# Small matmul groups of attention gathered into fewer places between weight chunks

## The chip, the cores and the metric

The kernel runs on one core of a Trainium2 chip. The metric is the device time of one execution in microseconds (us). TensorE (PE) multiplies matrices, ScalarE (ACT) and VectorE (DVE) work on its results and on its operands, SyncE (SP) issues transfers. Each of them runs its own list of instructions in order; an instruction waits where it needs another engine's result or a buffer that is not free yet.

## The reference

One layer of a hybrid decoder trunk on 256 positions of width 2048, in fp32. A convolution branch and differential attention share one input projection and one output projection; then come a 4-head cross attention to 256 memory tokens and a gated feed-forward part. What the change touches is the attention and the preparation of the memory tokens:

```python
logits = einsum("bqnd,bknd->bnqk", q_blk, k) * scale + bias      # 8 heads, two maps each
p = softmax(where(causal, logits, NEG_INF))
w = p[:, :, 0] - lam * p[:, :, 1]                                # one weight matrix per head
d = einsum("bhqk,bkhe->bqhe", w, v)                              # values
d = rms_norm(d, subln_g) * (1.0 - lambda_init)                   # per head, then reshaped
x = x + concatenate([a, d]) @ w_out
m = rms_norm(mem, g_mem); ckv = m @ w_ckv                        # memory tokens
x = x + cross_attention(rms_norm(x, g_cross) @ w_cq, ckv) @ w_co
x = x + (silu(u1) * u2) @ w_down                                 # u: hf @ w_up, then a short convolution
```

## The kernel before

Each fp32 operand of a large product is split into two parts: a rounded one ("hi", a cast on ScalarE, L162) and the rest ("lo", a subtraction on VectorE, L163). Three products of these parts stand for the fp32 product. Weights come in chunks of 512 KB, 128 x 1024; `weight` (from L144 on) issues the transfer and makes hi and lo. Raw, hi and lo have four buffers each, so the cast of a chunk needs the hi buffer of the chunk four before it, that is the end of that chunk's matmuls.

One chunk is twelve wide matmuls (L216, `part_a`), and this is called a step. At the end of each step `stage()` runs what was planned for it with `at(step, ...)`. So the small matmuls of attention stand in groups behind the last wide matmul of a chunk. Steps 32 to 39 are the first half of the values' projection (v0), 40 to 71 q and k of four pairs of heads (qk0 to qk3), 72 to 79 the second half of the values (v1), 80 to 87 and 88 to 95 the memory tokens' keys (ck) and values (cv), and from 96 on the output projection (wo).

The order on TensorE is the order of the code. On the other engines a scheduler places each instruction by its own simulation of the timeline, so a change of the code's order also moves theirs.

Small work of one head, in order: `turn` transposes q and k (L462, L463) and copies them (L465, qkT); `scores` multiplies them (L474, L477, lg), adds the bias on VectorE and takes exponentials on ScalarE (L487, L); `combine` transposes the head's weights (L506, wt) and copies them (L508, wT); `values` multiplies them with v (L519 to L521, o), and ScalarE reads the result four times, twice to scale and twice to square (L524, L526, jk); `sub_turn` scales the normed output (L540), transposes it (L541, oT) and splits it into the mix (L180, L181). The tiles wt, qkT, o, oT, and those of the two norms and of the memory keys' transposes, share two PSUM buffers (tag "sm", L83), so each needs the one two before it to have been read. lg has one buffer.

The table STEPS (L53) gives the step of each planned piece, the table PAIR (L59) the offset from the pair's base 48 + 8b of `turn`, `scores` and `combine` for the pair's two heads. Token rows of the memory for its norm (L573, row00 to row11) and quarters of the memory (L560, mem0 to mem3) are transfers of 512 KB on the same queue as the weights, into four buffers that they share with the attention's outputs (tag "h4"); a row is squared in place on ScalarE (L574), a quarter is split (L180, L181).

Of the kernel before, what the change touches and what calls it, by code (L numbers as in the profile page):

```python
# [27 lines left out]
NH = 8  # L28
# [14 lines left out]
for _name, _w in (("g_mix", KT), ("g_mem", KT), ("g_cross", KT), ("g_ffn", KT), ("caw", CT * TAPS),  # L43
# [8 lines left out]

STEPS = dict(x_square=(2, 4, 7, 8), x_add=(5, 7, 9), stats=9, gated=(12, 22, 24, 36), bias=43, lam=46,  # L53
             mem_load=(56, 59, 65, 70), mem_split=(68, 80), mem_square=(78, 72, 75, 81), mem_stats=85,
             mem_turn=(95, 89), ln_sum=80, ln_mean=85, ln_var=89, ln_norm=91,
             values=(59, 60, 67, 67, 81, 88, 85, 84), sub_scale=(69, 92), sub_turn=(72, 75, 90, 80, 94, 95, 92, 95),
             cross_scale=131, cross_logits=132, cross_turn=134, cross_values=135)

PAIR = ((2, "turn", 0), (3, "scores", 0), (3, "turn", 1), (4, "scores", 1), (10, "combine", 1), (8, "combine", 0))  # L59

RATES = ((0, 3.8), (36, 4.1), (46, 3.4))
AHEAD = (3, 0)
# [5 lines left out]
def trunk_kernel(ctx, tc, xT_d, memT_d, mem_d, par_d, tab_d, hot_d, gf_d, wa_d, wck_d, wv_d, wqk_d,  # L68
# [63 lines left out]
    def at(i, f, *args):  # L132
        assert i >= step[0]
        plan.setdefault(i, []).append(partial(f, *args))
# [409 lines left out]
    def attend(b, qk):  # L544

        for i, f, n in PAIR:
            i, hd = 48 + 8 * b + i, 2 * b + n
            if f == "turn":
                at(i, turn, hd, qk)
            else:  # L550
                at(i, scores if f == "scores" else combine, hd)
# [46 lines left out]
    for b in range(2):  # L598
        attend(b, pair(b))
# [5 lines left out]
    for f in (flush, ln_sum):  # L605
        at(STEPS["ln_sum"], f)
    attend(2, pair(2))
    attend(3, pair(3))
    at(STEPS["ln_mean"], ln_mean)
    at(STEPS["ln_var"], ln_var)  # L610
# [415 lines left out]
```

## Time and profile before

| | us |
|---|---|
| median of three runs (lowest, highest) | 1184.17 (1183.75, 1185.91) |
| the profiled execution | 1182.44 |
| its span, first to last instruction | 1180.7 |
| TensorE busy in the span | 1169.5 (99%) |
| VectorE, ScalarE busy | 927.0 (79%), 711.0 (60%) |
| TensorE's share of the chain that ended last | 98% |

The span is the profiled execution without some 1.7 us around it. In a timeline each row is an instruction, or several alike one after another ("x3"), with its start and duration; the brackets at the end of a row tell how long the engine stood idle before it and whose instruction ended that. Matmuls overlap, so what one costs is read from the start of one row to the start of the next.

### The profile page before, as it was taken

To read this page: it belongs to the slowest core of one execution; us is meant where nothing else is said; L and a number is where in the kernel's file an instruction comes from. 1 tells how busy PE (TensorE), PEld (TensorE's weight loads), DVE (VectorE), ACT (ScalarE), POOL (GpSimd) and SP (SyncE) were. 2 spreads that over 40 slices of the span, in tenths; PEclk is the share of its full clock that TensorE was granted. 3 is DMA by queue.
4 is the path that set the end of the run, shared out by engine and by line. 5 is a ranking of instruction groups with operands and counts; after the bars stand their busy time and mean duration, and the time that the engine had idled before them with its cause. 6 is when DMAs were issued, how large, how long until landed. Compare 5 with 4: busy or idle time off the path is not lost.

```text
span 1180.7 us, 17026 instructions
## 1 busy us (share of the span) xinstructions
PE 1169.5 (99%) x6186; PEld 1000.3 (85%) x6186; DVE 927.0 (79%) x1503; ACT 711.0 (60%) x1144; POOL 6.2 (1%) x16
## 2 busy tenths in 40 slices
PE   9999999999999999999999999999999999999997
PEld 7888888788888898888888888888888888888886
DVE  7899999996766687978778778778778877777773
ACT  8654467978655665755555555555555756555553
POOL 0000000000000000000000000000000000000000
PEclk9999999999999999999999999999999999999999
DMA  8756766664666547666566666666666566666663
GB/s 323 220 188 194 199 179 205 214 203 154 195 189 190 176 129 228 185 192 193 183 192 193 185 193 190 186 195 188 189 194 185 188 191 186 196 185 191 195 192 111
DMA packets 64032, 226.33 MB, mean 192 GB/s; under 512 B 7659, under 2 KB 8460, under 8 KB 63820
## 3 DMA queue, kind: packets, MB, share of 16 engines
q1 hardware_dynamic: 62732, 223.25, 60.8%
q0 software_dynamic: 784, 1.34, 0.5%
q8 instruction: 48, 0.79, 0.3%
q10 hardware_dynamic: 432, 0.66, 0.2%
q14 instruction: 36, 0.29, 0.1%
HBM read 222.83 MB, written 2.38 MB: 191 GB/s over the span
## 4 chain that ended last, share of the span: by engine, by line
PE 98%; DMA 1%; ACT 1%; DVE 0%; issue 0%; SPq 0%
PE up L197 27%; PE up L198 14%; PE qk L216 7%; PE a L216 7%; PE acc L846 7%; PE acc L848 7%; PE acc L847 7%; PE wo L197 5%; PE v L216 4%; PE wo L198 3%; PE cv L216 2%; PE ck L216 2%; PE cq L197 1%; PE wc L754 1%; PE cq L198 1%; PE wc L755 1%
## 5 line engine op out<-in xcount | busy, mean ns | idle before, releaser
L197 PE MATMUL up<-hf,hi_up 128*128 128x512 f32 x1408 | 488.3, 391 | 0.0
L198 PE MATMUL up<-hf,lo_up 128*128 128x256 f32 x1408 | 393.9, 280 | 0.0
L197 PEld LDWEIGHTS up<-hf,hi_up 128*128 128x128 f32 x1408 | 263.2, 187 | 57.7
L162 ACT CAST hi_up<-raw_up 128x1024 fp32r<-128x1024 f32 x176 | 185.5, 1054 | 149.3 <-PE up L197 107.6
L163 DVE TENSOR_TENSOR lo_up<-raw_up,hi_up 128x1024 fp32r<-128x1024 f32 x176 | 215.6, 1225 | 74.9 <-ACT hi_up L162 66.5
L198 PEld LDWEIGHTS up<-hf,lo_up 128*128 128x128 f32 x1408 | 266.0, 189 | 0.2
L846 PE MATMUL acc<-hi_dn,gq 128*128 128x512 f32 x352 | 137.3, 390 | 0.0
L848 PE MATMUL acc<-hi_dn,gq 128*128 128x512 f32 x352 | 137.0, 389 | 0.0
L847 PE MATMUL acc<-lo_dn,gq 128*128 128x512 f32 x352 | 137.0, 389 | 0.0
L163 DVE TENSOR_TENSOR lo_dn<-raw_dn,hi_dn 128x1024 fp32r<-128x1024 f32 x88 | 107.9, 1226 | 25.2 <-ACT hi_dn L162 24.9
L347 DVE SCALAR_TENSOR_TENSOR y<-ga,par,y 128x249 f32<-128x249 f32 (+17 forms) x240 | 99.4, 467 | 0.0
L162 ACT CAST hi_dn<-raw_dn 128x1024 fp32r<-128x1024 f32 x88 | 92.1, 1047 | 7.9 <-PE acc L848 6.4
L197 PE MATMUL wo<-mix,hi_wo 128*128 128x512 f32 x256 | 89.3, 395 | 0.0
L216 PE MATMUL qk<-hi_qk,h 128*128 128x512 f32 x256 | 82.3, 394 | 0.0
L216 PE MATMUL a<-hi_a,h 128*128 128x512 f32 x256 | 79.6, 392 | 1.1 <-ACT h L180 1.1
L848 PEld LDWEIGHTS acc<-hi_dn,gq 128*128 128x128 f32 x352 | 66.1, 188 | 13.9
L847 PEld LDWEIGHTS acc<-lo_dn,gq 128*128 128x128 f32 x352 | 66.1, 188 | 13.6
L846 PEld LDWEIGHTS acc<-hi_dn,gq 128*128 128x128 f32 x352 | 66.1, 188 | 13.5
L838 ACT CAST gq<-g_a 128x512 fp32r<-128x512 f32 x64 | 39.4, 623 | 58.6 <-PE acc L847 58.6
L198 PE MATMUL wo<-mix,lo_wo 128*128 128x256 f32 x256 | 70.6, 278 | 0.0
L228 ACT COPY corr_up<-up 128x256 f32<-128x256 f32 x88 | 32.7, 372 | 61.6 <-PE up L198 61.6
L839 DVE TENSOR_TENSOR gq<-g_a,gq 128x512 fp32r<-128x512 f32 x64 | 44.0, 691 | 27.4 <-ACT gq L838 27.4
(261 smaller groups left out, 1747.1 us busy)
## 6 DMA issues: line engine op xcount, KB each, us to landing
raw_up<-in_wup SPq DMA_DIRECT2D x176, 512.0 KB, 4.2
raw_dn<-in_wdn SPq DMA_DIRECT2D x88, 512.0 KB, 3.5
raw_qk<-in_wqk SPq DMA_DIRECT2D x32, 512.0 KB, 3.7
raw_wo<-in_wo SPq DMA_DIRECT2D x32, 512.0 KB, 3.6
raw_a<-in_wa SPq DMA_DIRECT2D x30, 512.0 KB, 4.2
raw_v<-in_wv SPq DMA_DIRECT2D x16, 512.0 KB, 3.5
raw_ck<-in_wck SPq DMA_DIRECT2D x8, 512.0 KB, 3.9
raw_cv<-in_wck SPq DMA_DIRECT2D x8, 512.0 KB, 3.6
```

The lines of the kernel that those rows point to most:

```text
L162: rounded = A.copy(out=hi, in_=raw)
L163: fill(rounded, V.tensor_tensor(out=lo, in0=raw, in1=hi.bitcast(F32), op=ALU.subtract))
L197: T.matmul(tiles[n], hi[:, o:o + P], acts(k), start=begin, stop=False)
L198: T.matmul(tiles[n][:, 0:S] if narrow else tiles[n][:, S:], lo[:, o:o + P], acts(k)[:, 0:S], start=False, stop=end)
L216: T.matmul(tiles[t], a, b[:, w], start=k + j == 0, stop=k == KT - 1 and j == 2)
L228: A.copy(out=c, in_=pst[:, S:])
L347: V.scalar_tensor_tensor(out=y[:, j, s:], in0=gated[j][:, 0:S - s], scalar=w, in1=y[:, j, s:], op0=ALU.mult, op1=ALU.add)
L838: A.copy(out=g[:, :, 0:S], in_=src)
L839: V.tensor_tensor(out=g[:, :, S:], in0=src, in1=g[:, :, 0:S].bitcast(F32), op=ALU.subtract)
L846: T.matmul(acc[t], ah, hi, start=False, stop=False)
L847: T.matmul(acc[t], ah, lo, start=False, stop=False)
L848: T.matmul(acc[t], al, hi, start=False, stop=c == NC - 1 and kk == 1)
```

## The change

Two tables of steps change. The transposes of the weights of a pair's even head move from offset 8 to 11, that is next to the scores of the following pair, and to 10 for the last pair, where they join those of the odd head. The values of heads come in twos: steps 60, 68, 80 and 84 in place of 59, 60, 67, 67, 81, 88, 85 and 84. The transposes of outputs move to 76, 76, 85, 89, 93, 93, 94 and 94, the scalings to 70 and 88, and one transpose of the memory keys from 89 to 91.

```diff
--- before.py
+++ after.py
@@ -52,11 +52,11 @@
 
 STEPS = dict(x_square=(2, 4, 7, 8), x_add=(5, 7, 9), stats=9, gated=(12, 22, 24, 36), bias=43, lam=46,
              mem_load=(56, 59, 65, 70), mem_split=(68, 80), mem_square=(78, 72, 75, 81), mem_stats=85,
-             mem_turn=(95, 89), ln_sum=80, ln_mean=85, ln_var=89, ln_norm=91,
-             values=(59, 60, 67, 67, 81, 88, 85, 84), sub_scale=(69, 92), sub_turn=(72, 75, 90, 80, 94, 95, 92, 95),
+             mem_turn=(95, 91), ln_sum=80, ln_mean=85, ln_var=89, ln_norm=91,
+             values=(60, 60, 68, 68, 80, 80, 84, 84), sub_scale=(70, 88), sub_turn=(76, 76, 85, 89, 93, 93, 94, 94),
              cross_scale=131, cross_logits=132, cross_turn=134, cross_values=135)
 
-PAIR = ((2, "turn", 0), (3, "scores", 0), (3, "turn", 1), (4, "scores", 1), (10, "combine", 1), (8, "combine", 0))
+PAIR = ((2, "turn", 0), (3, "scores", 0), (3, "turn", 1), (4, "scores", 1), (10, "combine", 1), (11, "combine", 0))
 
 RATES = ((0, 3.8), (36, 4.1), (46, 3.4))
 AHEAD = (3, 0)
@@ -544,7 +544,7 @@
     def attend(b, qk):
 
         for i, f, n in PAIR:
-            i, hd = 48 + 8 * b + i, 2 * b + n
+            i, hd = 48 + 8 * b + min(i, 10 if b == NH // 2 - 1 else 11), 2 * b + n
             if f == "turn":
                 at(i, turn, hd, qk)
             else:
```

In TensorE's list the places with small work of steps 50 to 95 become 21 from 27. The wide matmuls stay as they were. On the other engines the scheduler orders the same instructions anew; the transfer of mem1 and its four splits move from the attention's end to the first phase, behind mem0, and all other pieces stay within a few steps.

On ScalarE from step 74 on, before: `row01` and `row10` are squares of token rows, `qkT6` and `qkT7` the copies of `turn`, `wT5` a copy of `combine`, `mix2` with `oT1` an output's split.

```order
L162 CAST hi_v1_6_2330<-raw_v1_6_2328 128x1024
L508 COPY wT5_2187<-wt5_2183 128x384
L465 COPY qkT6_2194<-qkT6_2189 128x512
L574 ACTIVATE row01_2135,part_888<-row01_2135 128x1024
L162 CAST hi_v1_7_2354<-raw_v1_7_2352 128x1024
L180 ACTIVATE mix2_885<-oT1_2218,par_69 128x256
L574 ACTIVATE row10_2257,part_888<-row10_2257 128x1024
L465 COPY qkT7_2255<-qkT7_2250 128x512
```

The same stretch now.

```order
L162 CAST hi_v1_6_2330<-raw_v1_6_2328 128x1024
L574 ACTIVATE row01_2122,part_888<-row01_2122 128x1024
L508 COPY wT5_2174<-wt5_2170 128x384
L465 COPY qkT6_2181<-qkT6_2176 128x512
L540 ACTIVATE o4_0_1709<-o4_0_1709,ro0_2055 128x128 x8
L162 CAST hi_v1_7_2354<-raw_v1_7_2352 128x1024
L508 COPY wT4_2209<-wt4_2205 128x384
L574 ACTIVATE row10_2243,part_888<-row10_2243 128x1024
L465 COPY qkT7_2241<-qkT7_2236 128x512
```

The eight scalings of outputs (L540) and the copy wT4 came in ahead of qkT7's copy, and the output's split left. The transfer of row10 is now released by the square of row01; before, it was released by the splits of mem2 on VectorE.

On ScalarE up to the scaled values (L400, which the values of heads 4 to 7 read), before.

```order
L574 ACTIVATE row00_2349,part_888<-row00_2349 128x1024
L162 CAST hi_ck_0_2381<-raw_ck_0_2379 128x1024
L487 ACTIVATE L6_0_2232,st6_0_2234<-L6_0_2232,st6_0_2234 128x128 x2
L487 ACTIVATE L6_1_2241,st6_1_2243<-L6_1_2241,st6_1_2243 128x256 x2
L162 CAST hi_ck_1_2445<-raw_ck_1_2443 128x1024
L487 ACTIVATE L7_0_2289,st7_0_2291<-L7_0_2289,st7_0_2291 128x128 x2
L162 CAST hi_ck_2_2478<-raw_ck_2_2476 128x1024
L487 ACTIVATE L7_1_2298,st7_1_2300<-L7_1_2298,st7_1_2300 128x256 x2
L400 ACTIVATE v_882<-v1_0_2097,rx_tok_98 128x512
L643 ACT_TABLE_LOAD
L643 ACTIVATE warm_90<-st7_1_2300 128x1
L400 ACTIVATE v_882<-v1_1_2098,rx_tok_98 128x512
```

And now, from the first output's split (oT0) on; ahead of these rows, behind qkT7's copy, stand the table load, the exponentials of head 6 and the cast hi_ck_0.

```order
L180 ACTIVATE mix2_885<-oT0_2268,par_69 128x256
L180 ACTIVATE m2_2400<-mem2_1846,par_69 128x256 x4
L180 ACTIVATE m3_2417<-mem3_2066,par_69 128x256
L180 ACTIVATE mix2_885<-oT1_2275,par_69 128x256
L180 ACTIVATE m3_2417<-mem3_2066,par_69 128x256 x3
L574 ACTIVATE row00_2349,part_888<-row00_2349 128x1024
L487 ACTIVATE L7_0_2289,st7_0_2291<-L7_0_2289,st7_0_2291 128x128 x2
L162 CAST hi_ck_1_2454<-raw_ck_1_2452 128x1024
L487 ACTIVATE L7_1_2298,st7_1_2300<-L7_1_2298,st7_1_2300 128x256 x2
L162 CAST hi_ck_2_2475<-raw_ck_2_2473 128x1024
L400 ACTIVATE v_882<-v1_0_2097,rx_tok_98 128x512
L400 ACTIVATE v_882<-v1_1_2098,rx_tok_98 128x512
```

The eight splits of mem2 and mem3 (L180) moved in here; before they stood ahead of the cast hi_v1_6.

On ScalarE around the weights' copies of the last pair, before.

```order
L162 CAST hi_ck_4_2520<-raw_ck_4_2518 128x1024
L180 ACTIVATE mix2_885<-oT3_2400,par_69 128x256
L508 COPY wT6_2441<-wt6_2437 128x384
L162 CAST hi_ck_5_2548<-raw_ck_5_2546 128x1024
L162 CAST hi_ck_6_2599<-raw_ck_6_2597 128x1024
L508 COPY wT7_2498<-wt7_2494 128x384
L162 CAST hi_ck_7_2617<-raw_ck_7_2615 128x1024
L524 ACTIVATE o4_4_2461<-o4_2463,st4_0_1939 128x128
L526 ACTIVATE jk4_0_2468,oss4_2462<-o4_2463,st4_0_1939 128x128
L524 ACTIVATE o4_4_2461<-o4_2463,st4_1_1948 128x128
L526 ACTIVATE jk4_1_2471,oss4_2462<-o4_2463,st4_1_1948 128x128
L162 CAST hi_cv_0_2641<-raw_cv_0_2639 128x1024
```

Now.

```order
L162 CAST hi_ck_5_2561<-raw_ck_5_2559 128x1024
L162 CAST hi_ck_6_2609<-raw_ck_6_2607 128x1024
L524 ACTIVATE o4_4_2430<-o4_2432,st4_0_1919 128x128
L526 ACTIVATE jk4_0_2437,oss4_2431<-o4_2432,st4_0_1919 128x128
L524 ACTIVATE o4_4_2430<-o4_2432,st4_1_1928 128x128
L526 ACTIVATE jk4_1_2440,oss4_2431<-o4_2432,st4_1_1928 128x128
L524 ACTIVATE o4_4_2430<-o5_2442,st5_0_1992 128x128
L526 ACTIVATE jk5_0_2447,oss4_2431<-o5_2442,st5_0_1992 128x128
L524 ACTIVATE o4_4_2430<-o5_2442,st5_1_2001 128x128
L526 ACTIVATE jk5_1_2450,oss4_2431<-o5_2442,st5_1_2001 128x128
L508 COPY wT7_2495<-wt7_2491 128x384
L508 COPY wT6_2501<-wt6_2497 128x384
```

The reads of heads 4 and 5 (`o4_4` is the tile of heads 4 to 7's outputs) moved ahead of the copies wT7 and wT6, and stand behind the cast hi_ck_6.

On TensorE at the end of chunk ck_2, step 82, before.

```order
L216 MATMUL ck1_2378<-hi_ck_2_2478,m1_2106 128x512
L506 MATMUL wt7_2494<-ident_75,L7_0_2289 128x128
L506 MATMUL wt7_2494<-ident_75,L7_1_2298 128x128 x2
L216 MATMUL ck0_2377<-hi_ck_3_2502,m1_2106 128x512
L216 MATMUL ck0_2377<-lo_ck_3_2503,m1_2106 128x512
```

Now.

```order
L216 MATMUL ck1_2378<-hi_ck_2_2475,m1_2106 128x512
L506 MATMUL wt7_2491<-ident_75,L7_0_2289 128x128
L506 MATMUL wt7_2491<-ident_75,L7_1_2298 128x128 x2
L506 MATMUL wt6_2497<-ident_75,L6_0_2218 128x128
L506 MATMUL wt6_2497<-ident_75,L6_1_2227 128x128 x2
L216 MATMUL ck0_2377<-hi_ck_3_2505,m1_2106 128x512
```

Behind wt7 there is now wt6, which stood at step 80 before; the values of heads 4 and 5, whose buffers these two take, stand at the end of step 80.

## Rows read from the trace of the kernel before

**Rows 1.** The page: busy times with their share, and the clock in 40 slices.
```profile
PE 1169.5 (99%) x6186; PEld 1000.3 (85%) x6186; DVE 927.0 (79%) x1503; ACT 711.0 (60%) x1144; POOL 6.2 (1%) x16
...
PEclk9999999999999999999999999999999999999999
```

**Rows 2.** All waits of TensorE: us in total, times, longest.
```profile
PE a L216 <- ACT h L180: 1.1, 1, 1.1
...
PE qkT L462 <- ACT jk L526: 0.2, 1, 0.2
```

**Rows 3.** ScalarE's timeline, steps 82 to 84: start, us, instruction, [idle before, releaser].
```profile
255.24 1.05 ACT L162 CAST hi_ck<-raw_ck 128x1024 fp32r<-128x1024 f32 x1 [2.38 <-PE ck L216]
...
258.32 1.05 ACT L162 CAST hi_ck<-raw_ck 128x1024 fp32r<-128x1024 f32 x1 [1.66 <-PE ck L216]
259.28 0.36 ACT L524 ACTIVATE o<-o,st 128x128 f32<-128x128 f32 x1
...
260.38 0.21 ACT L526 ACTIVATION_READ_ACCUMULATOR jk<-o,st 128x1 f32 x1
```

**Rows 4.** ScalarE's timeline, steps 71 to 80.
```profile
217.43 2.44 ACT L540 ACTIVATE o<-o,ro 128x128 f32<-128x128 f32 x8
...
224.40 1.71 ACT L180 ACTIVATE m<-mem,par 128x256 fp32r<-128x256 f32 x4
...
229.86 0.48 ACT L508 COPY wT<-wt 128x384 f32<-128x384 f32 x1
...
233.80 1.06 ACT L574 ACTIVATE row<-row 128x1024 f32<-128x1024 f32 x1 [0.20 <-DMA row<-in_mem]
...
234.85 0.57 ACT L465 COPY qkT<-qkT 128x512 f32<-128x512 f32 x1
237.30 1.06 ACT L574 ACTIVATE row<-row 128x1024 f32<-128x1024 f32 x1 [1.87 <-DMA row<-in_mem]
...
238.35 1.04 ACT L162 CAST hi_ck<-raw_ck 128x1024 fp32r<-128x1024 f32 x1
239.30 0.39 ACT L487 ACTIVATE L<-L,st 128x128 f32<-128x128 f32 x1
...
241.06 1.04 ACT L162 CAST hi_ck<-raw_ck 128x1024 fp32r<-128x1024 f32 x1
...
245.11 0.69 ACT L400 ACTIVATE v<-v,rx_tok 128x512 f32<-128x512 f32 x1
245.81 1.28 ACT L643 ACT_TABLE_LOAD   x1
```

**Rows 5.** TensorE's timeline, steps 74 to 83.
```profile
228.40 0.49 PE L506 MATMUL wt<-ident,L 128*128 128x128 f32 x3
...
236.43 0.49 PE L474 MATMUL lg<-qkT 64*128 64x128 f32 x4
...
248.31 0.38 PE L541 MATMUL oT<-ident,o 128*128 128x128 f32 x2
...
252.20 0.47 PE L216 MATMUL ck<-hi_ck,m 128*128 128x512 f32 x1
252.51 0.39 PE L216 MATMUL ck<-lo_ck,m 128*128 128x512 f32 x1
...
255.04 0.49 PE L506 MATMUL wt<-ident,L 128*128 128x128 f32 x3
255.28 0.48 PE L216 MATMUL ck<-hi_ck,m 128*128 128x512 f32 x1
```

**Rows 6.** ScalarE's timeline, first phase.
```profile
32.08 1.05 ACT L162 CAST hi_a<-raw_a 128x1024 fp32r<-128x1024 f32 x1 [0.99 <-DMA raw_a<-in_wa]
34.46 1.05 ACT L162 CAST hi_a<-raw_a 128x1024 fp32r<-128x1024 f32 x1 [1.33 <-PE a L216]
```

**Rows 7.** The DMA queue's timeline, the transfers of token rows.
```profile
229.78 0.33 SPq L573 DMA_DIRECT2D row<-in_mem  x1
...
231.90 0.33 SPq L573 DMA_DIRECT2D row<-in_mem  x1
```

## Prediction

> **What bounds the kernel now.** I read the page first, then the list of TensorE's waits, then the timelines of TensorE, ScalarE and the DMA queue around the steps that the change touches. The page has TensorE busy for 1169.5 of 1180.7 us and its granted clock at full level in every slice [rows 1]. Its longest wait is 1.1 us, at the very start; in the whole attention part it waits once, 0.2 us for a PSUM buffer [rows 2]. So the work in front of TensorE is hidden today, and a change can win only what stands on TensorE itself, and lose whatever it uncovers on ScalarE, VectorE and the queue. The reader is to see in each timeline how near the cover is to its end: on ScalarE the casts of weights wait in brackets for TensorE, which means that ScalarE is ahead there [rows 3], and elsewhere it runs without a gap [rows 4].
>
> **The change part by part.** All small instructions stay; 27 groups of them become 21.
>
> *What is removed.* After a group the first wide matmul takes 0.31 us to the next one (252.20 to 252.51) against 0.23 in the ordinary rhythm (252.51 to 255.04 is eleven of them) [rows 5]. That is at most 0.08 per group, 0.5 for six; a group's own first instruction overlaps the matmul before it, so some of it stays within the larger group, and I take half, 0.25. The one wait of 0.2 [rows 2] goes too, because there values of a pair stood directly ahead of a turn and no longer do. Sum -0.45, carried on as -0.4, between 0 and -0.7.
>
> *Moved early.* The transfer of a quarter of the memory tokens (mem1) now stands before a weight chunk of the first phase, and its four splits before a cast there. Four splits are 1.71 us, as at 224.40 [rows 4]. In that phase ScalarE waits 0.99 us for a weight transfer and, two casts later, 1.33 for TensorE to free a buffer [rows 6]: it is a full round of four buffers ahead, and that cast's chunk is multiplied three chunks of about 2.8 us later. A delay of 1.7 to 3 us is inside that. I take 0, bounds 0 and 0.5.
>
> *Steps 58 to 72.* Values of heads 0 to 3 move back by at most a step and meet no tighter neighbour; the scaling of outputs leaves ScalarE's path at 217.43 (2.44 for the eight) [rows 4] and comes back in step 75. I take 0.
>
> *Step 76.* Here the second output transpose and the scores of head 7 wait for the copy of head 7's transposed q and k (qkT7), since outputs and qkT share two PSUM buffers. Before that copy ScalarE now has, in order: cast hi_v1_6, square of row01, copies wT5 and qkT6, eight scalings, cast hi_v1_7, copy wT4, square of row10. The cast follows the end of step 74's matmuls (228.40 in the trace) [rows 5] by 0.20, as 255.24 does 255.04 [rows 3, 5]. Then 0.95 (238.35 to 239.30) + 1.05 (233.80 to 234.85) + 0.4 + 0.5 (copies of 0.48 and 0.57, each 0.1 into the next) + 2.44 + 0.95 + 0.4 + 1.05 + 0.57 [rows 4] = 8.5 us after that end. Also row10's transfer now waits until row01's square is done, 2.2 after the end, and takes 4.0 (229.78 to 233.80) to 5.4 (231.90 to 237.30) [rows 4, 7]; with its square and the copy behind it, that path ends after 7.8 to 9.2. TensorE reaches the second transpose 8.35 after the same end: 228.40 to 236.43 is 8.03 [rows 5], and wt4 in place of an output transpose and one more transpose ahead add 0.3. Wait 0.15 to 0.9. I take 0.6; bounds 0 (the transfer quick, ScalarE a little ahead) and 2.0 (the transfer another 1 us late, as row00's was against row10's).
>
> *Step 80.* The values of heads 4 and 5 need the scaled v (L400), and now stand at the end of step 80 where head 4's stood one step later and head 5's eight. ScalarE reaches those two instructions, counted from the end of the qkT7 copy, after: table load 1.28, exponentials of head 6 1.76 (239.30 to 241.06), cast 0.95, eight splits of mem2 and mem3 3.3, two of the mix 0.75, square of row00 1.05, exponentials of head 7 1.76, two casts 1.9, v 0.69 = 13.4, and the second v 0.6 later, 14.0 [rows 4]. The splits are what is new: they ran at 224.40 to 229 in before [rows 4], in time that nobody waited for. TensorE gets there 0.3 (the second output transpose, a row of 0.38 that overlaps the next) + (248.31 - 236.43 = 11.88) = 12.2 after the same copy [rows 5]. The first matmuls wait 1.2, the ones on the second v a little more. I take 1.3; bounds 0 (the copy done earlier than TensorE wants it) and 2.5 (each of the 20 instructions 0.05 slower).
>
> *Step 82, the main term.* wT7's and wT6's transposes go behind chunk ck_2 as a pair, and take the two PSUM buffers that the values of heads 4 and 5 filled. Those are free when ScalarE has read them: four instructions per head. In its new order these eight stand behind the cast hi_ck_6, and hi_ck_6 needs the buffer of hi_ck_2, that is the last matmul of chunk ck_2, the very one ahead of wt7. So nothing can overlap: in the trace that cast starts 0.20 after that matmul's end, having waited 2.38 us for it [rows 3]. Cast 0.96 (258.32 to 259.28), four reads 1.31 (259.28 to 260.38 and 0.21) [rows 3]: TensorE idles 0.20 + 0.96 + 1.31 = 2.47, does wt7 in 0.32 (0.24 to the next wide matmul and 0.08 off that one) [rows 5], and waits for the next four reads, 1.31 - 0.32 = 0.99. Sum 3.4. It hangs on no duration that could shrink to nothing, only on this order. Bounds 2.5 (the second head's reads partly done) and 3.8. Behind it nothing is late: the next casts are for chunks four steps on.
>
> *Sum.* -0.4 + 0 + 0.6 + 1.3 + 3.4 = +4.9 us on the profiled execution's 1182.44, so 1187.3. That execution is 1.7 us under the median of the runs (1184.17); the same +4.9 on the median gives 1189.1, and I say 1189.0.
>
> [...] Before the change TensorE's gaps are 1.1 us at most, and the clock stays at full level over them [rows 1, 2]; a gap of 2.5 us, then 0.32 of work, then 1.0 is in no row. [...]
>
> **The rivals.**
> - *Not slower: the reads of heads 4 and 5 are done before wt7 is due.* If hi_ck_6 did not wait for the end of chunk ck_2, ScalarE, which has nothing else to do there, would read both buffers during step 81 and 82, some 5.5 us for 2.6 us of work. Step 82 then costs nothing, and what is left is -0.4 with 0 to 1.9 of the other two steps: 1183.8 to 1185.7. It decides when the reads end less than 0.32 after the last matmul of ck_2. For it: all such reads are hidden in before, and the brackets of 2.38 and 1.66 show slack on ScalarE [rows 3]. Against it: the bracket at 255.24 names exactly this matmul.
> - *The clock falls at step 82.* Eleven wide matmuls take 2.53 at full level [rows 5]; at half of it a chunk of twelve takes some 2.8 us more. One chunk: 1189.0 + 2.8 = 1191.8. For it: the longest gap of the kernel; against it: all gaps so far.
> - *Only step 82 costs.* If row10 lands in 4.0 us and the copy of qkT7 is early, steps 76 and 80 fall under the cover: 1184.17 - 0.4 + 3.4 = 1187.2.
> - *The early mem1 transfer delays the first phase.* The bracket of 0.99 for a weight transfer [rows 6] becomes some 2.5, and VectorE's half of that chunk is late: at most that 1.5 on the forecast, 1190.5.
>
> **How the numbers follow.** Chances: forecast 0.52, only step 82 0.20, clock 0.12, not slower 0.12, early transfer 0.04. The likeliest one's own range is 1187.5 to 1190.5 (steps 76 and 80 from 0.8 to 3.5 in place of 1.9, step 82 from 3.0 to 3.8). The range for 8 in 10 takes in "only step 82" with its lower bound and the clock: 1186.0 to 1192.3. Within 0.2% (2.4 us, about what a measurement of this kernel can tell from no change) reaches to 1186.5 and holds the first rival and a corner of the third: 0.14. Faster than 1181.8 would need over three times the most that the rows allow for the removed groups and the removed wait: 0.03. Slower: 0.83.
>
> **What would show it.** In the changed kernel's list of waits, TensorE should wait at wt7 (L506) for ScalarE's last read of head 4 about 2.5 us, at wt6 for head 5's about 0.9, at the values of head 4 (L519 to L521) for the second v about 1.3, and at an output transpose (L541) or head 7's scores (L474) for qkT7's copy about 0.6; TensorE's busy time should fall by some 0.3. If wt7 does not wait, the main term is wrong and the first rival holds; if the granted clock drops in the slice around step 82, the second. A wait at a weight chunk for VectorE's low half would mean that I overlooked VectorE.

## The result and the profile after

The changed kernel takes 1193.23 us (median of five executions, 1192.33 to 1194.79) against 1183.75 (1183.35 to 1185.91) for the kernel before on the same chip: a ratio of 1.0083 with an interval of [1.0071, 1.0095], +9.5 us. I forecast 1189.0, +4.9 us, in a range of 1186.0 to 1192.3. The direction was right; the size was half, and the time lies above the range. The profiled execution after takes 1192.63 us, its span is 1190.9.

The page's row of busy times, which answers to [rows 1]:

```profile
PE 1174.8 (99%) x6186; PEld 1004.5 (84%) x6186; DVE 927.3 (78%) x1503; ACT 711.5 (60%) x1144; POOL 6.2 (1%) x16
```

The same 6186 instructions keep TensorE busy 5.3 us longer than before. I expected 0.3 less. Of that 1.3 lies in the first 20 us (18.36 against 17.08), in a start that is told below. Each new gap also costs something beside its idle time, as the steps below show: 0.24 at step 76 (1.19 for a gap of 0.95), 0.39 at step 80 (1.27 for 0.88), 0.47 for the two of step 82 (3.49 for 3.02). For what is left the clock is a suspect. It can't be seen on the page's row of 40 slices, which still shows 9 in each: a slice is 30 us long.

All waits of TensorE from 0.6 us on, after (us in total, times, longest), for [rows 2]:

```profile
PE wt L506 <- ACT jk L526: 3.0, 2, 2.4
PE wo L197 <- DVE mix L178: 1.7, 2, 1.4
PE busy L105 <- DVE ones L99: 1.1, 1, 1.1
PE oT L541 <- ACT qkT L465: 0.9, 1, 0.9
PE o L519 <- ACT v L400: 0.9, 1, 0.9
PE a L216 <- ACT h L180: 0.6, 1, 0.6
```

Rows one, four and five are the three waits that I named, at the lines that I named. Row two, at the output projection, is nowhere in the prediction. TensorE's timeline after, around row one's (start, us, instruction, [idle before, releaser]):

```profile
258.30 0.39 PE L216 MATMUL ck<-hi_ck,m 128*128 128x512 f32 x1
261.05 0.55 PE L506 MATMUL wt<-ident,L 128*128 128x128 f32 x3 [2.36 <-ACT jk L526]
262.26 0.55 PE L506 MATMUL wt<-ident,L 128*128 128x128 f32 x3 [0.66 <-ACT jk L526]
262.56 0.48 PE L216 MATMUL ck<-hi_ck,m 128*128 128x512 f32 x1
...
264.01 0.63 PE L216 MATMUL ck<-lo_ck,m 128*128 128x512 f32 x1
```

And ScalarE's in the same stretch, which answers to [rows 3]:

```profile
258.73 1.04 ACT L162 CAST hi_ck<-raw_ck 128x1024 fp32r<-128x1024 f32 x1 [1.66 <-PE ck L216]
259.68 0.36 ACT L524 ACTIVATE o<-o,st 128x128 f32<-128x128 f32 x1
...
260.78 0.21 ACT L526 ACTIVATION_READ_ACCUMULATOR jk<-o,st 128x1 f32 x1
...
261.96 0.24 ACT L526 ACTIVATION_READ_ACCUMULATOR jk<-o,st 128x1 f32 x1
```

The reader is to see the chain that makes the stall: the last matmul of chunk ck_2 (258.30) releases the cast hi_ck_6 (258.73); behind it stand head 4's reads, the last of them at 260.78, which release wt7 at 261.05, and head 5's, the last at 261.96, which release wt6 at 262.26. Where that chunk's last wide matmul took 0.39, single ones behind the stall take up to 0.63 (264.01).

I work the ledger with the length of a step, from the first wide matmul of one chunk to that of the next, so that a gap, its restart and a slower chunk all count once. An undisturbed step of the same content comes from the experiments below (3.98, 2.84), or is an estimate from before's step and the rhythm of the transposes that were added to it (4.22, 3.27).

| term | forecast | measured | from |
|---|---|---|---|
| six groups and one wait of 0.2 gone | -0.4 | -0.2 | steps 32 to 76, without the wait of step 76 |
| step 76, output transpose behind qkT7's copy | +0.6 | +1.2 | 5.41 against 4.22 |
| step 80, values behind the second v | +1.3 | +1.3 | 5.25 against 3.98 |
| step 82, wt7 and wt6 | +3.4 | +3.5 | 6.76 against 3.27 |
| chunk 83 at a lower clock | rival, 2.8 | +1.6 | 4.43 against 2.84 |
| output projection's first chunk | none | +2.1 | experiments 3 and 9 |
| sum | +4.9 | +9.4 | |

The sum is also what lies between the start of step 4 and the first matmul of `up`: 432.09 us after, 422.69 before (the rounded rows add up to 9.5). The two profiled executions differ by 10.2 us: these 9.4, less 0.3 behind `up`, and 1.1 for a later start of step 4 (17.93 against 19.02), made in steps 0 to 3, which the change doesn't touch. The start of step 4 lies between 17.5 and 20.5 over the profiled executions here, and the changed kernel alone has 18.48, 19.02 and 20.46 (experiments 11 and 10 beside this one), so I don't put it down to the change, though of before there is only one trace. Part of it is the clock: in experiment 10 the granted clock is 0.78 and 0.79 in the stretches from 12 to 20 us.

The clock, in a table of TensorE's stretches after (stretch, length, busy time of PE, PEld, DVE, ACT, POOL with instructions, granted clock, DMA share, GB/s):

```profile
259.00:262.50 3.50, 0.79 (x5) 0.55 (x6) 3.47 (x5) 3.50 (x14) 0.00 (x0) 1.00 0.91 337
262.50:264.00 1.50, 1.50 (x7) 1.19 (x6) 0.91 (x2) 0.56 (x2) 0.00 (x0) 0.68 0.99 396
264.00:265.50 1.50, 1.50 (x5) 1.20 (x4) 0.00 (x0) 0.43 (x1) 0.00 (x0) 0.50 0.87 317
265.50:267.00 1.50, 1.50 (x6) 1.17 (x6) 0.45 (x3) 0.92 (x3) 0.00 (x0) 0.68 0.20 79
267.00:268.50 1.50, 1.50 (x8) 1.27 (x7) 0.92 (x6) 1.05 (x1) 0.00 (x0) 1.00 0.00 0
```

After a stretch with 0.79 us of work in 3.5, the granted clock is 0.68, 0.50 and 0.68 in the three stretches up to 267.00, and then 1.00 again. TensorE has no gap there: it is busy for 1.50 of 1.50 in each, and the chunk takes 1.6 us longer (4.43 against 2.84), which no list of waits shows.

### The profile page after: what moved, and what is told of

The parts are those of the page before. It is cut to its first block, busy times and chain, and to the rows that moved or that the text cites. A ratio compares the mean times of both kernels' runs of the same rounds, so it can differ in the third digit from the quotient of the medians.

```text
span 1190.9 us, 17025 instructions
## 1 busy us (share of the span) xinstructions
PE 1174.8 (99%) x6186; PEld 1004.5 (84%) x6186; DVE 927.3 (78%) x1503; ACT 711.5 (60%) x1144; POOL 6.2 (1%) x16
## 4 chain that ended last, share of the span: by engine, by line
PE 95%; ACT 3%; DMA 1%; issue 0%; DVE 0%; ACTq 0%
PE up L197 27%; PE up L198 14%; PE a L216 8%; PE qk L216 7%; PE acc L847 7%; PE acc L846 7%; PE acc L848 7%; PE wo L197 5%; PE v L216 3%; PE wo L198 2%; PE ck L216 2%; PE cq L197 1%; PE cv L216 1%; PE cq L198 1%; PE wc L754 1%; PE wc L756 1%
## 5 line engine op out<-in xcount | busy, mean ns | idle before, releaser
L197 PE MATMUL up<-hf,hi_up 128*128 128x512 f32 x1408 | 488.3, 391 | 0.0
L197 PEld LDWEIGHTS up<-hf,hi_up 128*128 128x128 f32 x1408 | 263.2, 187 | 57.7
L197 PE MATMUL wo<-mix,hi_wo 128*128 128x512 f32 x256 | 89.3, 392 | 1.7 <-DVE mix L178 1.7
```

Source lines behind the costliest of these rows:

```text
L197: T.matmul(tiles[n], hi[:, o:o + P], acts(k), start=begin, stop=False)
```

## The experiments

All are edits of the changed kernel (the numbers are those of their labels; there is no 8); each median stands beside the kernel before on the same chip in the same job, and two kernels of different jobs are compared by their differences from it. The changed kernel's is +9.5. Where the clock falls, what it costs differs from one execution to the next (1.0 to 2.8 us in the traces below), so medians here scatter by more than a microsecond, and I read small differences from the steps of the traces.

**1. Values of heads 4 and 5 at their old steps.** My theory: step 82 stalls because ScalarE reads their buffers too late. The rival: the pair of wt7 and wt6 costs this wherever the buffers stand.

```diff
-             values=(60, 60, 68, 68, 80, 80, 84, 84), ...
+             values=(60, 60, 68, 68, 81, 88, 84, 84), ...
```

> Values of heads 4 and 5 back to steps 81 and 88, all else as changed (1193.2 us). Theory: the stall of step 82 (3.5 us by the chunk's length) exists only because wt7 and wt6 take the buffers of o4 and o5, so it falls below 1 us and the slow chunk behind it (1.6) goes with it; the wait of step 80 (1.3) is not the values' own but ScalarE's and VectorE's lateness behind the eight splits, so it moves to the low half of chunk ck_1, which VectorE ended at 252.3 where TensorE would want it at 250.7: 1.6. Sum 1193.2 - 3.0 - 1.6 + 0.3 = 1188.9. Rival 1: the wait of step 80 is the values' own and goes: 1187.3. Rival 2: the stall of step 82 has another cause and stays: about 1192.

Measured: 1189.48 against 1183.13, 1.0053 [1.0038, 1.0068]. TensorE's waits:

```profile
PE ck L216 <- DVE lo_ck L163: 1.5, 1, 1.5
PE wt L506 <- ACT wT L508: 1.1, 1, 1.1
```

The wait for L526 is gone, and with it the slow chunk (step 83: 2.83). Step 82 falls from 6.76 to 4.84, not to 3.3: wt6 now waits for wt7's copy (L508). And the wait for the second v didn't vanish: with the values out of its way, chunk 81 waits 1.50 for VectorE's lo_ck_1. The theory on the stall holds, but the rival has a part in it: 1.6 of the 3.5 stay with the pair. The chain is nearly the same: wT7's copy (258.18 on ScalarE) stands behind the cast hi_ck_6 (257.23), which waits for the end of chunk ck_2, and wt6 starts behind that copy (258.71), before head 4's reads end (259.27). So wt6 takes wt7's own buffer here, and not that of the tile two before, as the description of the kernel has it. The 1.3 of step 80 only changes place.

**2. wt7 and wt6 one step later, at step 83.** Does a chunk more of cover free both?

```diff
-  i, hd = 48 + 8 * b + min(i, 10 if b == NH // 2 - 1 else 11), 2 * b + n
+  i, hd = 48 + 8 * b + ((11 if i > 9 else i) if b == NH // 2 - 1 else i), 2 * b + n
```

> The weights' transposes of heads 7 and 6 one step later, behind chunk ck_3, all else as changed (1193.2). Theory: the reads of heads 4 and 5 run beside chunk ck_3, so wt7 waits for nothing; in this order one of the eight reads, the last of head 5, stands behind the next cast, hi_ck_7, which needs the end of chunk ck_3, so wt6 waits 0.2 + 0.95 + 0.4 - 0.3 = 1.2, and after so short a gap the clock holds: 1193.2 - 3.5 - 1.6 + 1.2 = 1189.3. Rival 1: the slow chunk behind has nothing to do with the stall's length: 1190.9. Rival 2: the stall only moves by a step: 1193.

Measured: 1190.96 against 1183.13, 1.0065 [1.0050, 1.0080]. TensorE's timeline:

```profile
261.64 0.55 PE L506 MATMUL wt<-ident,L 128*128 128x128 f32 x3 [1.46 <-ACT jk L526]
...
266.20 0.49 PE L519 MATMUL o<-v,wT 128*128 128x128 f32 x2 [1.26 <-ACT wT L508]
```

ScalarE's:

```profile
264.63 1.06 ACT L574 ACTIVATE row<-row 128x1024 f32<-128x1024 f32 x1 [2.67 <-DMA row<-in_mem]
```

wt7 is free and only wt6 waits; the clock holds (0.999 over this trace's span; steps 83 and 84 take 4.98 and 5.61, and the waits with their restarts explain the excess). But wT6's copy now stands behind a token row's square that waits 2.67 for its transfer, and the values of step 84 pay 1.26. I had missed that. By the steps it is 1.6 (5.61 against 3.98), about the 1.7 by which the median lies over what I expected.

**3. Scaling and output transposes of heads 4 to 7 at their old steps.** This tests the wait that I hadn't foreseen.

```diff
-             ... sub_scale=(70, 88), sub_turn=(76, 76, 85, 89, 93, 93, 94, 94),
+             ... sub_scale=(70, 92), sub_turn=(76, 76, 85, 89, 94, 95, 92, 95),
```

> Output transposes of heads 4 to 7 back to 94, 95, 92, 95 and their scaling to 92, all else as changed (1193.2). Theory: the wait of the output projection's first chunk for its first operand (1.4 and 0.3 in the list, 2.1 by the chunks) comes from ScalarE's order there, in which all eight normalisations of the convolution branch stand ahead of the first casts, and that order comes from the moved transposes; it goes: 1191.1. Rival: ScalarE is late there because of the stalls before; then it stays: 1193.2.

Measured: 1189.10 against 1183.13, 1.0048 [1.0031, 1.0064]. No wait at L197 is left in its list, while the stall and the slow clock stay (steps 82 and 83: 7.01 and 3.97). From the first matmul of the memory values to the first of `up` it takes 169.24 us, after 171.19: 1.95 less, about the 2.1 of the ledger. The median lies another 2 us under what I expected; by the mean granted clock of its four executions (0.996, 0.996, 0.999, 0.998) two of them lost less to the clock than this trace, or nothing.

**4. Eleven more wide matmuls ahead of wt7.** Their result is read by nobody; they fill the gap without shortening it. If the slow chunk comes from the clock, it should go; if it comes from something behind the reads (late weights, the transfers beside it), it should stay.

```diff
+        if hd == NH - 1:
+            fl = lg_ps("fill")
+            for k in range(11):
+                T.matmul(fl[:, 0, :], m(k % 4)[:, 0:P], m(k % 4)[:, 0:2 * S], start=True, stop=True)
```

> Eleven wide matmuls whose result nobody reads stand ahead of wt7 at step 82 (2.5 us of work in the first part of the stall, 2.4 us), all else as changed (1193.2). Theory: the four chunks' worth of slow matmuls behind the stall are the granted clock, which fell because TensorE stood idle; with the gap filled it stays at full level, the chunk after takes 2.84 in place of 4.43 us, and the reads end when they did: 1193.2 - 1.6 = 1191.6. Rival 1: the slow chunk comes from the stall in another way (refilling, transfers), and stays: 1193.2. Rival 2: the filler delays the rest: above 1194.

Measured: 1191.11 against 1183.13, 1.0066 [1.0051, 1.0081]. Its stretches:

```profile
259.00:262.00 3.00, 2.33 (x14) 1.65 (x13) 2.96 (x4) 2.92 (x14) 0.00 (x0) 1.00 0.98 366
262.00:264.00 2.00, 2.00 (x11) 1.66 (x10) 0.72 (x2) 0.48 (x1) 0.00 (x0) 1.00 0.92 295
```

Step 82 keeps its length (6.763 against 6.755), chunk 83 takes 2.84 instead of 4.43, and the DMA share is as high as after's. So chunk 83 was slow because TensorE had idled, not for its operands. By the medians, each against before in its own job, it is worth 1.5 (+9.5 to +8.0).

**5. Four of them.**

```diff
-            for k in range(11):
+            for k in range(4):
```

> As the run with eleven unread matmuls ahead of wt7, with four (0.9 us of work), so that TensorE stands idle 1.5 us ahead of wt7 and 0.7 ahead of wt6. Theory: a gap of 1.5 us is one over which the clock held in two runs of this study, so it holds, the chunk behind takes 2.84, and the time is that of the run with eleven: 1191.3. Rival: the clock falls for the sum of both gaps (2.1 of 3.3 us): the slow chunk is back, up to 1193.2.

Measured: 1192.32 (1190.05 to 1195.33) against 1183.42, 1.0072 [1.0048, 1.0095]. A miss. Its stretches:

```profile
260.00:262.00 2.00, 0.55 (x3) 0.31 (x3) 2.00 (x2) 2.00 (x12) 0.00 (x0) 1.00 0.95 371
262.00:264.00 2.00, 1.94 (x7) 1.65 (x8) 1.16 (x3) 0.86 (x3) 0.00 (x0) 0.60 0.85 281
```

Behind gaps of 1.46 and 0.67 the clock fell (0.60 here and 0.55 in the 2 us after; chunk 83: 4.43), behind experiment 2's gap of 1.46 alone, and then 1.26 a chunk later, it did not. Not every execution loses by it: the mean granted clocks of the four are 0.997 (this trace), 0.998, 0.996 and 0.999.

**6. The splits of mem2 and mem3 eight steps earlier.** I had put step 80's wait down to these splits.

```diff
-             ... mem_split=(68, 80), ...
+             ... mem_split=(68, 72), ...
```

> The second half of the memory tokens' splits is planned at step 72 in place of 80, all else as changed (1193.2). In this order ScalarE has the eight splits of mem2 and mem3 earlier, not between qkT7's copy and v. Theory: the wait of step 80 (1.3 us) is made by these splits and falls to 0.4 or less; ScalarE is later at step 76, where the output transposes wait 1.7 and some more in place of 1.2; the stall of step 82 and the slow chunk stay. Sum 1193.2 - 0.9 + 0.9 = 1193.2, and the waits tell it. Rival: v is late whatever stands ahead; then step 80 waits 1.3 as before.

Measured: 1191.55 against 1183.42, 1.0064 [1.0048, 1.0079]. Its waits at L541:

```profile
PE oT L541 <- ACT qkT L465: 1.4, 1, 1.4
PE oT L541 <- ACT wT L508: 0.3, 1, 0.3
```

Step 80 takes 3.98, without a wait, so the splits were its cause. But they now stand ahead of qkT7's copy: step 76 takes 7.10 instead of 5.41, and chunk 77 behind it 3.67 instead of 2.88, in the manner of chunk 83. In this trace nothing was won; the work only changed its victim. It is the slowest of the four executions (1193.12) and has the lowest mean granted clock (0.995); the others, with 0.997 and 0.998, take 1189.50 to 1192.04, so the median is better than after's by 1.4 against before.

**7. The first two output transposes at step 77.**

```diff
-             ... sub_turn=(76, 76, 85, 89, 93, 93, 94, 94),
+             ... sub_turn=(77, 77, 85, 89, 93, 93, 94, 94),
```

> The output transposes of heads 0 and 1 one step on, from 76 to 77, all else as changed (1193.2). Theory: the copy of qkT7 itself is late on ScalarE (eight scalings ahead of it, and a transfer of a token row that lands 5.3 us after its issue), so without the transposes the scores of head 7 wait for it in their place, 1.2 us, and nothing is won: 1193 to 1194.5. Rival: the wait comes from the transposes' place, two tiles on one PSUM buffer pair; then it goes: 1192.0.

Measured: 1195.03 against 1183.42, 1.0092 [1.0077, 1.0107]. Its waits:

```profile
PE o L519 <- ACT v L400: 2.3, 1, 2.3
PE wo L197 <- DVE mix L178: 1.7, 2, 1.4
PE lg L474 <- ACT qkT L465: 1.4, 1, 1.4
```

Without the transposes head 7's scores wait for the same copy, longer because TensorE arrives earlier. The late copy is the cause, not who asks for it. The wait at the values of step 80 grew as well, from 0.9 to 2.3 (step 80: 6.71 for 5.25), because in this order a table load stands ahead of v on ScalarE, which after has behind it:

```profile
249.93 1.28 ACT L643 ACT_TABLE_LOAD   x1
```

That gap of 2.33, with none near it, is nearly as long as that of step 82, and the chunk behind it takes 2.84, as long as behind experiment 4's filled gap, where the granted clock was 1.00.

**9. The last two output transposes at step 95 instead of 94.** The smallest edit against the output projection's wait.

```diff
-             ... sub_turn=(76, 76, 85, 89, 93, 93, 94, 94),
+             ... sub_turn=(76, 76, 85, 89, 93, 93, 95, 95),
```

> Only the output transposes of heads 6 and 7 go one step on, from 94 to 95 (still as a pair); all else as changed (1193.2). In the changed kernel TensorE's list has them and the weight chunk cv_7 behind the first chunk of the output projection, which waits 1.4 and 0.3 for its operands; here they stand behind cv_7 and cv_7 stands ahead of the output projection. Theory: the wait is that order on TensorE; ScalarE's order there is as it was, and the 2.7 us of cv_7 cover its lateness, so the wait goes, 2.06 by the chunks: 1191.1. Rival: ScalarE's eight normalisations ahead of the first casts are too late in any order, or lateness from the stalls before reaches to here; then it stays: 1193.2.

Measured: 1190.37 against 1183.42, 1.0051 [1.0036, 1.0066]. In after, twenty wide matmuls of the output projection (its first chunk and the beginning of the second) and the output transposes of heads 6 and 7 stand between the last wide matmul of chunk cv_6 and the first of cv_7. So the output projection's first chunk stands ahead of cv_7. In before, in experiment 3 and here, it stands behind it. The timeline after at that place:

```profile
300.81 0.39 PE L216 MATMUL cv<-hi_cv,m 128*128 128x512 f32 x1
302.60 0.50 PE L197 MATMUL wo<-mix,hi_wo 128*128 128x512 f32 x1 [1.40 <-DVE mix L178]
...
305.30 0.50 PE L197 MATMUL wo<-mix,hi_wo 128*128 128x512 f32 x1 [0.32 <-DVE mix L178]
...
306.80 0.60 PE L541 MATMUL oT<-ident,o 128*128 128x128 f32 x4
307.16 0.47 PE L216 MATMUL cv<-hi_cv,m 128*128 128x512 f32 x1
```

And in before, where cv_7's last wide matmul is followed by the projection:

```profile
295.29 0.39 PE L216 MATMUL cv<-hi_cv,m 128*128 128x512 f32 x1
295.51 0.39 PE L197 MATMUL wo<-mix,hi_wo 128*128 128x512 f32 x1
```

What the projection waits for in after is VectorE's half of the mix, which waits for ScalarE:

```profile
302.12 1.10 DVE L178 TENSOR_TENSOR mix<-y,mix 128x256 fp32r<-128x256 f32 x3 [4.42 <-ACT mix L177]
```

The same place in this experiment:

```profile
300.95 0.39 PE L216 MATMUL cv<-hi_cv,m 128*128 128x512 f32 x1
301.18 0.39 PE L197 MATMUL wo<-mix,hi_wo 128*128 128x512 f32 x1
```

With cv_7's 2.7 us ahead of it the projection follows in the ordinary rhythm of 0.23. The stretch up to `up` takes 169.11, 2.08 less than after. And one thing that I hadn't asked for: the stall at step 82 is the same, 2.36 and 0.67, but in this trace the clock stays at full level behind it, and chunk 83 takes 2.84:

```profile
257.00:261.00 4.00, 0.97 (x6) 0.51 (x6) 3.97 (x6) 3.74 (x14) 0.00 (x0) 1.00 0.89 312
261.00:263.00 2.00, 2.00 (x11) 1.70 (x11) 0.93 (x2) 0.60 (x2) 0.00 (x0) 1.00 0.90 266
```

That is this execution alone (1188.17, mean granted clock 0.999). The three others of the same kernel take 1190.35 to 1190.78, with 0.997, 0.995 and 0.997.

**10 and 11. The changed kernel again, unedited, twice,** to see whether the fall belongs to the kernel or to the execution.

> The changed kernel as it is, profiled a second time. Behind the same stall of step 82 (2.4 and 0.7 us of idle time) the next chunk was slow in five traces of this study and not in one (the run with the transposes of heads 6 and 7 at 95), and it was slow too where four unread matmuls shortened the gap to 1.5. Theory: whether the granted clock falls depends on where the gap falls in time, so over executions of one kernel the chunks behind the stall take 2.84 to 4.5 us, and all waits of TensorE stay within 0.3 us of the first profile. Rival: the stall's length alone decides, and the chunk takes 4.4 each time.

> The changed kernel a third time, as the run before: theory 2.84 to 4.5 us for the chunk behind the stall, with the waits as they were; rival 4.4 each time.

Measured: 1195.77 and 1195.78, beside 1183.19 for before. In the first, chunk 83 takes 4.20, in the second 5.27, where the clock is low for longer, as its stretches show:

```profile
262.00:264.00 2.00, 2.00 (x7) 1.71 (x8) 1.09 (x2) 0.80 (x2) 0.00 (x0) 0.50 0.94 340
...
266.00:268.00 2.00, 2.00 (x6) 1.52 (x6) 0.62 (x4) 1.21 (x3) 0.00 (x0) 0.50 0.04 16
```

The rival, 4.4 each time, is refuted; 5.27 lies over the range of the theory too, and that the gap's place in time decides was my estimate: no run shows what does. Over the eight traces with the stall (after, experiments 3, 6, 7, 9, 10, 11 and 13: a gap of 2.36, and a second of 0.67, 0.63 in 13 and 0.32 in 7) the loss behind it, by steps 82 to 84, is 0 once and 1.0 to 2.8 seven times. The mean granted clock, taken over the whole span and on record for every execution, says the same of more of them: of 27 executions of these kernels, 21 have 0.997 or less and six 0.998 or 0.999, while all 20 of experiments 1, 2, 4 and 12, which have the stall shortened, moved or filled, have 0.998 or 0.999 (before: 0.998 or 0.999 in all but one of 31). The fall belongs to the stall; whether it comes, and its length, to the execution.

**12. Experiments 1 and 9 together.**

```diff
-  values=(60, 60, 68, 68, 80, 80, 84, 84), ... sub_turn=(76, 76, 85, 89, 93, 93, 94, 94),
+  values=(60, 60, 68, 68, 81, 88, 84, 84), ... sub_turn=(76, 76, 85, 89, 93, 93, 95, 95),
```

> Two edits at once: values of heads 4 and 5 back at 81 and 88, and the output transposes of heads 6 and 7 at 95; all else as changed. Theory: each of the waits has a place and a cause of its own, so the gains add: the stall of step 82 falls to 1.6, the clock holds, the wait of step 80 stays as one for VectorE's low half (1.8), that of the output projection is gone: 1193.2 - 1.9 - 1.6 + 0.6 - 2.1 = 1188.2, and no wait of more than 0.3 us that these runs have not shown. Rival: lateness is handed on, and with the later wait gone another takes its place: 1190 as with either edit alone.

Measured: 1186.69 against 1183.19, 1.0032 [1.0021, 1.0043], the best version of the grouping. Its waits:

```profile
PE ck L216 <- DVE lo_ck L163: 1.5, 1, 1.5
PE wt L506 <- ACT wT L508: 1.1, 1, 1.1
...
PE oT L541 <- ACT qkT L465: 0.8, 1, 0.8
```

Two edits of one table take back 6.0 of the 9.5 us; by themselves they took back 3.1 and 2.5, so the causes add. The median lies 1.5 under what I expected; between step 4 and `up` this trace takes 5.0 less than after, as expected. The three waits left, with their restarts 1.7, 1.6 and 1.0 by the steps' lengths, make 4.3 of the 4.4 us by which it is still longer there than before. So no version beat before, and what the groups themselves save can't be told from nothing here.

**13. Only the later half of the change.** Everything up to step 75 as before, the grouping from step 80 on as after.

```diff
-  values=(60, 60, 68, 68, 80, 80, 84, 84), ... sub_turn=(76, 76, 85, 89, 93, 93, 94, 94),
+  values=(59, 60, 67, 67, 80, 80, 84, 84), ... sub_turn=(72, 75, 85, 89, 93, 93, 94, 94),
```

(the first scaling at 69 and the even head's combine at offset 8, except in the last pair, go with it)

> The change with its earlier part undone: values of heads 0 to 3, output transposes of heads 0 and 1, their scaling and the even heads' weights of the first three pairs are as before; what is changed from step 80 on stays. ScalarE's order up to v is then that of before, with the splits of mem2 and mem3 ahead of step 75. Theory: the waits of steps 76 and 80 (1.2 and 1.3 us) are made by the earlier edits, which let the order put the splits late, and are gone (at most 0.4 at step 80, where a table load stands between the two v); the stall of step 82 (3.5), the clock behind it (1 to 2.8) and the wait of the output projection (2.1) stay: 1183.2 + 3.5 + 1.6 + 2.1 - 0.2 = 1190.2. Rival: step 80's wait comes with the values' own move to step 80 and stays, 1191.5 or more.

Measured: 1190.87 against 1183.39, 1.0068 [1.0049, 1.0087]. Its waits:

```profile
PE wt L506 <- ACT jk L526: 3.0, 2, 2.4
PE wo L197 <- DVE mix L178: 1.7, 2, 1.4
```

Steps 76 and 80 take 3.78 and 3.98 without a wait. So both of those waits are made by the earlier half, step 80's too: there the splits had come late because the work ahead of them had. Steps 82 and 83 are as long as the longest seen (7.01 and 5.27).

## Where the prediction held and where it failed

*What is removed* was forecast at -0.4 and gave -0.2. The vanished wait of 0.2 is already all of that; a group's first instruction costs next to nothing.

*Moved early* and *steps 58 to 72* at 0 held: steps 4 to 31 take 78.06 us before and after, steps 32 to 71 123.65 and 123.53.

*Step 76* had the right wait and too small a size, 0.6 for 1.2. ScalarE's timeline after shows the order as predicted, with the row's transfer late:

```profile
235.25 0.47 ACT L508 COPY wT<-wt 128x384 f32<-128x384 f32 x1
236.51 1.06 ACT L574 ACTIVATE row<-row 128x1024 f32<-128x1024 f32 x1 [0.78 <-DMA row<-in_mem]
237.56 0.56 ACT L465 COPY qkT<-qkT 128x512 f32<-128x512 f32 x1
```

The row was issued on SyncE's queue at 231.24 and its square began at 236.51, 5.3 us later: the slow end of the 4.0 to 5.4 that I took from [rows 4, 7]. TensorE's wait follows ScalarE's wait for this row from trace to trace: 0.17 and 0.42 in experiment 9, 0.60 and 0.96 in experiment 1, 0.78 and 0.95 after, 0.91 and 1.19 in experiment 3. The other 0.24 are the restart, which the list of waits doesn't give.

*Step 80* was right (1.3), and its cause, the eight splits, is shown by experiment 6 (and by 13, where they stand ahead of step 75).

*Step 82*, the main term, was right to 0.1 (3.5 for 3.4), with its two gaps 2.36 and 0.66 where I worked out 2.47 and 0.99. That the sum comes out so near is in part luck: the gaps are 0.4 shorter than mine, and their restarts, which have no place in my working, make up for it. Experiment 1 confirms that the reads of heads 4 and 5 are what it waits for. The rival by which they would be done in time is refuted.

The first step that failed is the pricing of *the clock*. I saw that the stall would be the longest gap of the kernel, worked out 2.8 us for its consequence, gave it 0.12 and left it out of the sum, because the clock had stayed at full level over all gaps so far, of 1.1 at most. Those rows say nothing on a gap of 2.4. Nor did a row that I had read show the half clock that my 2.8 is worked out with. The traces do: it is 0.50 after in the stretch from 264.00, and before, at the end of the program, where the last matmul begins at 1172.63, it is 1.00 up to 1177.00, 0.78 up to 1179.00 and 0.50 from there to the end. Seven of the eight traces with this stall have a slow chunk behind it; the one of experiment 9 has none, nor has that of experiment 7 behind its gap of 2.33 at step 80. My price of 2.8 was the upper end of what came: 1.6 in this trace, 1.0 to 2.8 in the seven. With 1.6 in the sum I would have said 1190.6.

The second is a place that has no part in my working: *the output projection's first chunk*, +2.1. I followed the steps that the tables name and stopped at step 95. The description of the kernel says that TensorE's order is the order of the code; that holds up to the end of the memory values, where `manual.close()` stands (L641). The output projection is behind it in the code, and the scheduler may place it earlier. In all fourteen traces it puts twenty wide matmuls of the projection directly ahead of the last output transposes. Where those are planned at step 95, as in before (heads 5 and 7), in experiments 3, 9 and 12, the code has cv_7 ahead of them, and cv_7 covers the wait; where they are planned at 94, as after, cv_7 has to stay behind them, and so behind the projection. It stood in TensorE's list before any run, had I read that list to the end of the part that moved. Why the scheduler puts the projection just there I did not try.

The two together are what the sum lacked most. Either alone would have left it inside the range of 1186.0 to 1192.3 (1190.6 with the clock, 1191.1 with the projection); with both it is 1192.7, and the 0.6 that step 76 lacked brings it to 1193.3, while before's median came out 0.4 lower than the one that I started from. One sum of the prediction is wrong by itself: its likeliest case, with 3.5 and 3.8 at the upper end, reaches to 1191.1 and not to 1190.5.

What stays open: why the clock held in one trace out of eight, and by the mean clock in six executions of 27, with the same gaps and about the same DMA share (0.89 against 0.91).

## What to carry to other kernels

Where an engine is busy for 99% and hidden work stands behind it, gathering small work saves little (here 0.2 us for six groups and a wait) and takes cover from whatever it is gathered next to: for each moved piece, look at which instruction frees its buffer, and what stands ahead of that one on its own engine. When such a chain begins with the end of the very chunk that should cover it, expect the stall: here it came in each of the eight traces with that order, and its size could be added up from rows beforehand. Then price what a stall sets off (here a slower clock behind it, 0 to 2.8 us over the eight traces) in the sum and not as a remark, and read every engine's list up to where the two kernels agree again.

## What the runs showed of the hardware

The same gaps on TensorE (2.36 and mostly 0.67 us, 0.55 of work between them in after's trace) cost 0 to 2.8 us in clock afterwards, from one trace to the next: in after the granted clock goes down to 0.50 and the chunk behind takes 4.43, in experiment 9 it stays at 1.00 and the chunk takes 2.84. Whole times don't show this as scatter: in the first job the changed kernel's five executions spread over 2.5 us and those of before over 2.6.

The length of the longest gap alone did not decide in these traces. Some pairs of shorter gaps had a slower clock behind them too: 1.46 and 0.67 with 0.55 of work between (experiment 5; granted clock 0.60 and 0.55, chunk 83 in 4.43), 0.33 and 1.37 with 0.44 between (experiment 6, step 76; chunk 77 in 3.67 instead of 2.88), and 0.74 and 0.76 (experiment 10, in its first 16 us; 0.78 and 0.79 from 12 to 20). The gaps that stood by themselves had none: 1.50 in experiments 1 and 12 and 1.46 in experiment 2 (a mean granted clock of 0.999 in each of the three traces), and 2.33 in experiment 7 (the chunk behind it in 2.84).

And the start of the program, up to step 4, differs between executions of the same instructions: the changed kernel's three traces reach step 4 at 18.48, 19.02 and 20.46 us.
